# Scan of a hybrid backbone: the unit matrix and r are scaled on GpSimd and added on VectorE, not by identity products

## Chip, core and metric

One core of a Trainium2 chip runs the whole program. The metric is the device time of one execution in microseconds (us), the median of several runs. PE is the tensor engine (its weight loads are listed apart, as PEld), DVE the vector engine, ACT the scalar engine, POOL is GpSimd and SP issues DMAs.

## What is computed

Two trunk layers of a diffusion backbone over 512 latent and 256 context tokens of width 1024. Layer 0 has an RWKV-7 time mixer in both directions beside a windowed attention, layer 1 two kinds of attention; each layer has a squared-ReLU MLP. The change touches only the scan of the RWKV-7 mixer, which for each of 8 heads and 2 directions keeps a 64x64 state:

```python
def rwkv7_scan(f, d, s0, reverse):
    def step(state, inp):
        r_t, w_t, k_t, v_t, kk_t, a_t = inp
        sa = jnp.einsum('bhvk,bhk->bhv', state, -kk_t)
        state = (state * w_t[:, :, None, :] + sa[..., None] * (kk_t * a_t)[:, :, None, :]
                 + v_t[..., None] * k_t[:, :, None, :])
        return state, jnp.einsum('bhvk,bhk->bhv', state, r_t)
```

## The kernel before

The scan runs in chunks of 64 tokens: 12 chunks (4 of context, 8 latent), taken forwards and backwards at once, and two heads side by side on the 128 partitions, so there are four head pairs. For one pair, `prep` (lines 843 to 985) makes the factors of all chunks: AR holds four 64-column parts for each chunk (a of both directions, r of both directions, scaled by cumulative decays), BK the matching b and k, wc the decay over a whole chunk (one column for each, with one more column in front), and XI the inverse of a triangular matrix. That inverse is found on VectorE by 31 steps of two operations (lines 954 and 955, "the solver") and a merge on TensorE.

`chunks` (lines 989 to 1168) then makes one pass over the pair, in four blocks of NB = 3 chunks. In an iteration b, the helpers take turns between two neighbouring blocks: factors(b), local(b-1), masked(b), passed(b-1), own(b), step(b-1, 0), solved(b), step(b-1, 1), step(b-1, 2).

- `factors` transposes BK into BT, a into the right half of XA and v into Z; a copy of v (vr) is made in parts by ScalarE and GpSimd first.
- `masked` forms a·k (AK, masked on VectorE, line 1053) and the right half of BT (masked on VectorE, line 1060).
- `own` multiplies AK with v, `solved` multiplies by XI and overwrites the right half of XA with the solved a.
- `local` makes each chunk's own output (into py) and own state N.
- `passed` makes, for each chunk, M and Q, with which the state is passed on and read: M = 1 + (solved a)·b and Q = r + (solved a)·k, each then scaled by the chunk's decay wc along the row. The 1 and the r come into PSUM as products with the identity (lines 1110 and 1111: the constant i2, two 64x64 unit matrices on top of each other, and AR's r), in one accumulation with the products of XA and BT (line 1114); a helper `chain` keeps all of these in order on TensorE (its matmuls are recorded at lines 1012 and 1015). VectorE then reads PSUM, multiplies by wc and writes the tile MQ (line 1116). The first chunk of all has no state before it, so in a pass's first block only two of three chunks are done.
- `step` carries the state over a chunk with M (line 1131), adds N (line 1133), and adds the state's output with Q into py (line 1138).

The passes run one behind another, and a caller draws from three generators by rates: the pass, the preparation of the pairs behind it together with the output of the pair before (`mix_out`), and `ada`, which streams 512 KB pieces of modulation weights through TensorE (line 353). Each engine serves its own queue in order; how the queues are ordered was settled when the program was built, from the order in the code and from what is ready when. Tiles of one name share buffers: AK has one, MQ, XA, BT and Z have two each; AR, BK, XI and wc have one for each of two neighbouring pairs. On GpSimd run the copies of v (line 1038), the products with k (lines 940 and 947), the powers for norms (line 264, called from `pow_mhalf`), and the solver's unit matrix (lines 930 and 931).

Of the kernel before, what the change touches and what calls it, by code (L numbers as in the profile page):

```python
# [11 lines left out]
F32 = mybir.dt.float32  # L12
F32R = mybir.dt.float32r
AF = mybir.ActivationFunctionType
ALU = mybir.AluOpType
# [159 lines left out]
def trunk(ctx: ExitStack, tc: tile.TileContext, xT, cT, vec_d, wada, we, wo_in, wout, wf1, wf2, lw2_d, la2_d, lg2_d,  # L175
          rpb_d, con_d, nm_d, rot_d, out):
    nc = tc.nc
    V, S, G, PE = nc.vector, nc.scalar, nc.gpsimd, nc.tensor
    tt, ts, stt = V.tensor_tensor, V.tensor_scalar, V.scalar_tensor_tensor

    def act(o, i, f=AF.Copy, **k):
        return S.activation(o, i, f, **k)  # L182
# [12 lines left out]
    C = {k: con[:, s] for k, s in CON.items() if k != "tri"}  # L195
    VV = {k: vec[:, s] for k, s in VEC.items()}
    ident = C["ident"]
# [645 lines left out]
    def prep(p, R, rt, iv, sts, res):  # L843
# [4 lines left out]
        k = rt.tile([128, T], F32, name="k")  # L848
# [41 lines left out]
        XI = st.tile([128, NCH, 2, 64], F32, name="XI")  # L890
        xv = XI.rearrange("p c h t -> p (c h) t")
        wc = st.tile([128, 2, NCH + 1], F32, name="wc")

        AR = st.tile([128, NCH, 4, 64], F32, name="ar")
        BK = [st.tile([128, NCH, 128], F32, name=f"bk{d}") for d in range(2)]
# [25 lines left out]
        for d in range(2):  # L921
            for b in range(2):
                o = d * 64 + b * 32
                i0 = d * 48 + b * 24
# [25 lines left out]
        for s in range(31):  # L950
            a, b = s + 1, 31 - s
# [10 lines left out]
        for d in range(2):  # L962
            for b in range(2):
                o = d * 64 + b * 32
                i0 = d * 48 + b * 24
# [21 lines left out]
    NB = 3  # L987

    def chunks(p, y, ct, pch, res):
# [5 lines left out]
        AR, BK, XI, wc, kds = res[p]  # L995
        half = lambda q: slice(q * 64, q * 64 + 64)
# [5 lines left out]
        pd = pch.tile([128, 128], F32, name="pd")  # L1002
        yp = py[:, :, 0:384].rearrange("p h (c f) -> p h c f", f=64)
        B = [{} for _ in range(NCH // NB)]
        last = None
        env = {}

        def chain(*a, **k):

            nonlocal last  # L1010
            if last is None:
                last = PE.matmul(*a, **k)
            else:
                with tc.issue_after(last.ins):
                    last = PE.matmul(*a, **k)  # L1015

        def factors(b):

            pt = wide()[:, 0:NB * 256].rearrange("p (x h k) -> p h x k", x=2 * NB, h=2)
            BT = B[b]["BT"] = ct.tile([128, 2, 2 * NB, 128], F32, name="BT", bufs=2)  # L1020
            for d in range(2):
                for i in range(NB):
                    PE.transpose(pt[:, :, d * NB + i], BK[d][:, ch[d][NB * b + i], :], ident)
            act(BT[:, :, :, 0:64], pt)
            XA = B[b]["XA"] = ct.tile([128, NB, 2, 128], F32, name="XA", bufs=2)
            pw = wide()
            pt = pw[:, 0:NB * 128].rearrange("p (i h k) -> p i h k", i=NB, h=2)
            for i in range(NB):
                PE.transpose(pt[:, i], AR[:, NB * b + i, 0:2].rearrange("p d t -> p (d t)"), ident)
            pv = pw[:, 512:512 + NB * 128].rearrange("p (i f) -> p i f", i=NB)  # L1030
            vr = ct.tile([128, NB, 2, 64], F32, name="vr")
            c0 = BWD[NB * b + NB - 1]
            act(vr[:, ::-1, 0, ::-1], c3(v)[:, c0:c0 + NB])

            n = min(NB, max(4 - NB * b, 0)) or NB
            for i0, i1 in ((0, n), (n, NB)):
                if i0 < i1:
                    G.tensor_copy(vr[:, i0:i1, 1], c3(v)[:, FWD[NB * b + i0]:FWD[NB * b + i0] + i1 - i0])
            for i in range(NB):
                PE.transpose(pv[:, i], vr[:, i].rearrange("p d t -> p (d t)"), ident)  # L1040
            act(XA[:, :, :, 64:128], pt)
            Z = B[b]["Z"] = ct.tile([128, NB, 2, 2, 64], F32, name="Z", bufs=2)
            for d in range(2):
                act(Z[half(1 - d), :, d].rearrange("p i h v -> p i (h v)"), pv[half(1 - d)])
# [17 lines left out]
        def own(b):  # L1062

            AK, Z, XA = (B[b][x] for x in ("AK", "Z", "XA"))
            px = wide()[:, 0:NB * 128].rearrange("p (i h v) -> p i h v", i=NB, h=2)
            for i in range(NB):
                for h, d in HD:
                    PE.matmul(px[half(d), i, h], AK[half(1 - d), h, i], Z[half(1 - d), i, d, h], start=True, stop=True)
            act(XA[:, :, :, 0:64], px)

# [33 lines left out]
        def passed(b):  # L1104

            BT, XA = B[b]["BT"], B[b]["XA"]
            i0 = 0 if b else 1
            pm = wide().rearrange("p (d x) -> p d x", d=2)[:, :, 0:NB * 128].rearrange("p d (i k) -> p d i k", i=NB)
            for d in range(2):
                chain(pm[:, d, i0:, 0:64], ident, C["i2"].unsqueeze(1).to_broadcast([128, NB - i0, 64]), start=True, stop=False)  # L1110
                chain(pm[:, d, i0:, 64:128], ident, AR[:, NB * b + i0:NB * b + NB, 2 + d], start=False, stop=False)
            for i in range(i0, NB):
                for h, d in HD:
                    chain(pm[half(h), d, i], XA[half(d), i, h, 64:128], BT[half(d), h, d * NB + i], start=False, stop=i == NB - 1)
            MQ = B[b]["MQ"] = ct.tile([128, 2, NB, 128], F32, name="MQ", bufs=2)
            tt(MQ[:, :, i0:], pm[:, :, i0:], wc[:, :, NB * b + i0:NB * b + NB].unsqueeze(3).to_broadcast([128, 2, NB - i0, 128]), op=ALU.mult)

        X = None

# [350 lines left out]
    with ExitStack() as p2:  # L1470
# [28 lines left out]
        for p in range(4):  # L1499
# [32 lines left out]
            t = None  # L1532
# [215 lines left out]
    with ExitStack() as p3:  # L1748
# [13 lines left out]
        with pool("po", 1) as pp:  # L1762
            ws = [W.take() for _ in range(4)]
            po = [pp.tile([128, T], F32, name=f"po{m}") for m in range(6)]
            for ms, gs in ((range(4), GROUPS[:2]), ((4, 5), GROUPS[:2]), ((0, 1), GROUPS[2:])):
                for c, tok in gs:
                    while c == 1 and pend:
                        tick()
                    for m in ms:
                        if m == len(ws):  # L1770
                            ws.append(W.take())
                        p = product(ws[m], *u1, tok.start, tok.stop, 12)
# [119 lines left out]
```

## Time and profile before

| | us |
|---|---|
| median of 3 runs | 2055.58 |
| lowest and highest of them | 2053.28, 2057.93 |
| the profiled execution | 2050.14 |
| its span, first to last instruction | 2048.3 |
| the scan's four passes, in the span | about 352 to 692 |

The profile shows one execution. Its summary gives busy times by engine; a table by windows gives them by stage; lists of groups, of waits and a timeline give single instructions; the chain of waits follows the work that ended last back from the end. An fp32 product of the code appears as two records on PE and two weight loads on PEld. The tile b is the PSUM tile of the scan's products. An activation of ScalarE appears under line 182, whoever calls it. Not all records are there: a few matmuls can be missing.

### The profile page before, as it was taken

What the parts mean: (1) busy time and instruction counts of PE and PEld (TensorE: products, weight loads), DVE (VectorE), ACT (ScalarE), POOL (GpSimd) and SP (SyncE); (2) the same over time, 40 slices, a digit from 0 to 9 for tenths busy, and PEclk for the clock granted to TensorE, in tenths of its full rate; (3) what the DMA queues carried; (4) which work ended last, traced back from release to release, by engine and by line L of the source; (5) the groups of instructions that cost most, each with busy time, mean ns of one, the idle gap of its engine ahead of it and who ended that gap; (6) DMA issues with size and microseconds to landing.
All of it is one profiled execution on the core that took longest, in us unless ns stands there. A gap on an engine that the chain in (4) does not pass through costs nothing.

```text
span 2048.3 us, 38617 instructions
## 1 busy us (share of the span) xinstructions
PE 1929.7 (94%) x16412; PEld 1630.5 (80%) x16412; DVE 1124.1 (55%) x1999; ACT 816.5 (40%) x1531; POOL 124.1 (6%) x149
## 2 busy tenths in 40 slices
PE   5999989888888899999999999899999899999997
PEld 3878767565666898888888889898878798888887
DVE  6576477467465387233444345856575575444445
ACT  3466443434335354311322122435686654222332
POOL 1000011011100000000000000001021000000000
PEclk9999989988999999999999999999999999999998
DMA  7512334675744234211221021342111334222321
GB/s 311 162 52 78 108 116 148 205 200 190 199 134 138 71 121 133 72 53 41 83 72 62 32 83 42 103 153 67 58 32 37 124 113 165 93 83 82 100 86 42
DMA packets 112013, 217.47 MB, mean 106 GB/s; under 512 B 38496, under 2 KB 63968, under 8 KB 111328
## 3 DMA queue, kind: packets, MB, share of 16 engines
q1 hardware_dynamic: 96544, 191.66, 29.2%
q10 hardware_dynamic: 15296, 23.33, 3.2%
q8 instruction: 129, 2.11, 0.4%
q14 instruction: 44, 0.36, 0.1%
HBM read 184.29 MB, written 28.05 MB: 104 GB/s over the span
## 4 chain that ended last, share of the span: by engine, by line
PE 61%; DVE 5%; ACT 3%; issue 2%; DMA 2%; POOL 1%; POOLq 0%; ACTq 0%; DVEq 0%; SPq 0%
PE x L1589 46%; PE x L430 5%; PE ax L530 2%; PE ax L511 2%; PE b L493 1%; PE b L494 1%; PE b L1015 1%; DMA w_raw<-in_wada_dram 1%; PE b L1077 1%; DVE nacc L288 1%; PE ad L353 0%; ACT P L182 0%; DVE h L310 0%; ACT w_hi L182 0%; ACT Z L182 0%
## 5 line engine op out<-in xcount | busy, mean ns | idle before, releaser
L182 ACT ACTIVATE w_hi<-w_raw 128x1024 fp32r<-128x1024 f32 x183 | 192.3, 1058 | 480.7 <-PE x L1589 367.5
L225 DVE TENSOR_TENSOR w_lo<-w_raw,w_hi 128x1024 fp32r<-128x1024 f32 x181 | 220.9, 1223 | 196.1 <-ACT w_hi L182 194.4
L1589 PE MATMUL x<-fl,w_hi 128*128 128x256 f32 (+1 forms) x864 | 291.5, 339 | 3.9 <-DVE fl L1676 3.9
L1589 PE MATMUL x<-uh,w_hi 128*128 128x512 f32 (+1 forms) x864 | 287.6, 338 | 3.0 <-ACT uh L182 3.0
L1589 PE MATMUL x<-fh,w_lo 128*128 128x256 f32 (+1 forms) x864 | 289.8, 337 | 0.0
L1589 PE MATMUL x<-ul,w_hi 128*128 128x512 f32 (+1 forms) x864 | 287.9, 336 | 0.0
L1589 PE MATMUL x<-uh,w_lo 128*128 128x512 f32 (+1 forms) x864 | 287.5, 336 | 0.0
L1589 PE MATMUL x<-fh,w_hi 128*128 128x256 f32 (+1 forms) x864 | 287.3, 338 | 0.0
L1603 DVE TENSOR_TENSOR oa<-x,oa 128x512 f32<-128x512 f32 (+1 forms) x184 | 103.1, 563 | 207.6 <-PE x L1589 206.9
L430 PE MATMUL x<-uh,w_hi 128*128 128x256 f32 (+1 forms) x560 | 190.3, 340 | 1.0 <-ACT po L182 0.7
L430 PE MATMUL x<-uh,w_lo 128*128 128x256 f32 (+1 forms) x560 | 189.1, 338 | 0.0
L430 PE MATMUL x<-ul,w_hi 128*128 128x256 f32 (+1 forms) x560 | 188.3, 336 | 0.0
L1589 PEld LDWEIGHTS x<-fl,w_hi 128*128 128x128 f32 x864 | 165.0, 191 | 22.0 <-DVE fl L1676 4.5
L1589 PEld LDWEIGHTS x<-uh,w_hi 128*128 128x128 f32 x864 | 162.4, 190 | 21.2 <-ACT uh L182 3.9
L1589 PEld LDWEIGHTS x<-fh,w_lo 128*128 128x128 f32 x864 | 164.8, 191 | 17.8
L1589 PEld LDWEIGHTS x<-fh,w_hi 128*128 128x128 f32 x864 | 162.5, 190 | 19.9 <-ACT fh L182 2.5
L1589 PEld LDWEIGHTS x<-ul,w_hi 128*128 128x128 f32 x864 | 163.0, 190 | 17.7
L1589 PEld LDWEIGHTS x<-uh,w_lo 128*128 128x128 f32 x864 | 162.9, 189 | 17.6
L430 PEld LDWEIGHTS x<-uh,w_hi 128*128 128x128 f32 x560 | 107.6, 192 | 12.0 <-issue 2.7
L430 PEld LDWEIGHTS x<-uh,w_lo 128*128 128x128 f32 x560 | 107.7, 192 | 9.5 <-issue 1.2
L430 PEld LDWEIGHTS x<-ul,w_hi 128*128 128x128 f32 x560 | 107.8, 192 | 9.3 <-issue 1.3
L1675 DVE TENSOR_TENSOR rl<-rl 128x512 f32<-128x512 f32 (+1 forms) x108 | 59.3, 551 | 77.7 <-ACT fh L182 77.5
(304 smaller groups left out, 3388.7 us busy)
## 6 DMA issues: line engine op xcount, KB each, us to landing
w_raw<-in_wf_dram SPq DMA_DIRECT2D x128, 512.0 KB
w_raw<-in_wada_dram SPq DMA_DIRECT2D x96, 512.0 KB
w_raw<-in_we_dram SPq DMA_DIRECT2D x21, 512.0 KB
w_raw<-in_wo_in_dram SPq DMA_DIRECT2D x18, 512.0 KB
w_raw<-in_wout_dram SPq DMA_DIRECT2D x16, 512.0 KB
hsc<-h ACTq DMA_DIRECT2D x8, 1024.0 KB
scr<-po ACTq DMA_DIRECT2D x21, 384.0 KB
h<-hsc SPq DMA_DIRECT2D x7, 1024.0 KB
```

The source lines that it names most:

```text
L182: return S.activation(o, i, f, **k)
L225: eng.tensor_tensor(o_lo, x, o_hi.bitcast(F32), op=ALU.subtract)
L288: V.tensor_reduce(acc, sq.rearrange("p k t -> p t k"), axis=AX.X, op=ALU.add)
L430: PE.matmul(ps[:, 0:b - a], x, y, start=j == 0, stop=j == len(pairs) - 1)
L493: PE.matmul(ps[:, off:off + n], qs, kh, start=True, stop=False)
L494: PE.matmul(ps[:, off:off + n], qs, kl, start=False, stop=True)
L511: PE.transpose(pt[:, (kb - k0) * 128:(kb - k0 + 1) * 128], P[:, kb * 128:(kb + 1) * 128], ident)
L530: PE.matmul(po[h * 64:h * 64 + 64, 0:128], v(h, k), pts[h][:, k], start=k == 0, stop=k == n - 1)
L1015: last = PE.matmul(*a, **k)
L1589: PE.matmul(o, a, b, start=n == 0, stop=n == len(pairs) - 1)
L1603: tt(oa[:, m, tok], ps, oa[:, m, tok], op=ALU.add)
L1675: tt(r, r, r, op=ALU.mult)
```

## The change

The products with the identity go, and with them the helper `chain`. GpSimd gets three operations for each block, at the start of the block in `factors`: a times wc into a new tile, which takes its turn in AK's buffer and is transposed in place of a; the unit matrix times wc into the left halves of MQ; r times wc into its right halves. MQ is so taken up one iteration earlier than before. In `passed` TensorE makes only the products of XA and BT, already scaled by wc through a, and VectorE adds MQ to them and writes MQ. The first column of wc, which nobody read before, is set to 1.

```diff
--- before.py
+++ after.py
@@ -890,6 +890,7 @@
         XI = st.tile([128, NCH, 2, 64], F32, name="XI")
         xv = XI.rearrange("p c h t -> p (c h) t")
         wc = st.tile([128, 2, NCH + 1], F32, name="wc")
+        G.memset(wc[:, :, 0:1], 1.0)
 
         AR = st.tile([128, NCH, 4, 64], F32, name="ar")
         BK = [st.tile([128, NCH, 128], F32, name=f"bk{d}") for d in range(2)]
@@ -1002,17 +1003,7 @@
         pd = pch.tile([128, 128], F32, name="pd")
         yp = py[:, :, 0:384].rearrange("p h (c f) -> p h c f", f=64)
         B = [{} for _ in range(NCH // NB)]
-        last = None
         env = {}
-
-        def chain(*a, **k):
-
-            nonlocal last
-            if last is None:
-                last = PE.matmul(*a, **k)
-            else:
-                with tc.issue_after(last.ins):
-                    last = PE.matmul(*a, **k)
 
         def factors(b):
 
@@ -1022,11 +1013,19 @@
                 for i in range(NB):
                     PE.transpose(pt[:, :, d * NB + i], BK[d][:, ch[d][NB * b + i], :], ident)
             act(BT[:, :, :, 0:64], pt)
+
+            aw = ct.tile([128, NB, 2, 64], F32, name="AK")
+            w_ = wc[:, :, NB * b:NB * b + NB].unsqueeze(3).to_broadcast([128, 2, NB, 64])
+            di = lambda x: x.rearrange("p i d t -> p d i t")
+            G.tensor_tensor(di(aw), di(AR[:, NB * b:NB * b + NB, 0:2]), w_, op=ALU.mult)
+            IR = B[b]["MQ"] = ct.tile([128, 2, NB, 128], F32, name="MQ", bufs=2)
+            G.tensor_tensor(IR[:, :, :, 0:64], C["i2"].unsqueeze(1).unsqueeze(1).to_broadcast([128, 2, NB, 64]), w_, op=ALU.mult)
+            G.tensor_tensor(IR[:, :, :, 64:128], di(AR[:, NB * b:NB * b + NB, 2:4]), w_, op=ALU.mult)
             XA = B[b]["XA"] = ct.tile([128, NB, 2, 128], F32, name="XA", bufs=2)
             pw = wide()
             pt = pw[:, 0:NB * 128].rearrange("p (i h k) -> p i h k", i=NB, h=2)
             for i in range(NB):
-                PE.transpose(pt[:, i], AR[:, NB * b + i, 0:2].rearrange("p d t -> p (d t)"), ident)
+                PE.transpose(pt[:, i], aw[:, i].rearrange("p d t -> p (d t)"), ident)
             pv = pw[:, 512:512 + NB * 128].rearrange("p (i f) -> p i f", i=NB)
             vr = ct.tile([128, NB, 2, 64], F32, name="vr")
             c0 = BWD[NB * b + NB - 1]
@@ -1106,14 +1105,11 @@
             BT, XA = B[b]["BT"], B[b]["XA"]
             i0 = 0 if b else 1
             pm = wide().rearrange("p (d x) -> p d x", d=2)[:, :, 0:NB * 128].rearrange("p d (i k) -> p d i k", i=NB)
-            for d in range(2):
-                chain(pm[:, d, i0:, 0:64], ident, C["i2"].unsqueeze(1).to_broadcast([128, NB - i0, 64]), start=True, stop=False)
-                chain(pm[:, d, i0:, 64:128], ident, AR[:, NB * b + i0:NB * b + NB, 2 + d], start=False, stop=False)
             for i in range(i0, NB):
                 for h, d in HD:
-                    chain(pm[half(h), d, i], XA[half(d), i, h, 64:128], BT[half(d), h, d * NB + i], start=False, stop=i == NB - 1)
-            MQ = B[b]["MQ"] = ct.tile([128, 2, NB, 128], F32, name="MQ", bufs=2)
-            tt(MQ[:, :, i0:], pm[:, :, i0:], wc[:, :, NB * b + i0:NB * b + NB].unsqueeze(3).to_broadcast([128, 2, NB - i0, 128]), op=ALU.mult)
+                    PE.matmul(pm[half(h), d, i], XA[half(d), i, h, 64:128], BT[half(d), h, d * NB + i], start=True, stop=True)
+            MQ = B[b]["MQ"]
+            tt(MQ[:, :, i0:], pm[:, :, i0:], MQ[:, :, i0:], op=ALU.add)
 
         X = None
```

## Rows read from the trace of the kernel before

**Rows 1.** The summary: busy us (share of the span) x instructions.
```profile
PE 1929.7 (94%) x16412; PEld 1630.5 (80%) x16412; DVE 1124.1 (55%) x1999; ACT 816.5 (40%) x1531; POOL 124.1 (6%) x149
```
**Rows 2.** Busy us (x instructions) by window, one for each pass; header shows columns.
```profile
core 0: us, PE busy (x) PEld busy (x) DVE busy (x) ACT busy (x) POOL busy (x), PEclk, DMA share, GB/s
352.00:454.00 102.00, 89.48 (x1708) 61.95 (x1710) 60.16 (x133) 39.33 (x76) 11.83 (x11) 0.94 0.71 210
454.00:552.00 98.00, 87.30 (x1418) 60.54 (x1418) 55.14 (x124) 34.68 (x66) 10.36 (x11) 0.89 0.63 191
552.00:626.00 74.00, 63.62 (x1526) 49.33 (x1522) 45.07 (x107) 29.54 (x61) 7.34 (x8) 1.00 0.48 132
626.00:692.00 66.00, 56.31 (x1060) 46.95 (x1061) 30.98 (x41) 32.04 (x55) 4.95 (x5) 0.92 0.31 108
```
**Rows 3.** Waits from 352 to 692 us: total us, times, longest.
```profile
PE ad L353 <- DMA w_raw<-in_wada_dram: 9.0, 9, 1.8
PE pd L1131 <- DVE MQ L1116: 8.2, 10, 1.9
...
DVE ar L903 <- PE b L1015: 9.2, 2, 5.2
DVE y L1201 <- POOL r L264: 7.2, 3, 2.4
...
POOL vr L1038 <- PE b L1040: 85.9, 9, 24.6
```
**Rows 4.** Timeline of a block in the last pass: start, us, engine, line, operation.
```profile
674.55 0.59 PE L1015 MATMUL b<-con 128*128 128x192 f32 x2
674.64 0.96 DVE L1060 TENSOR_TENSOR BT<-b,con 128x768 f32<-128x768 f32 x1
...
676.05 0.89 PE L1015 MATMUL b<-BT,XA 64*64 64x128 f32 x24
...
677.01 0.96 DVE L1116 TENSOR_TENSOR MQ<-b,wc 128x768 f32<-128x768 f32 x1 [1.41 <-PE b L1015]
...
678.02 0.38 PE L1131 MATMUL pd<-x,MQ 64*64 64x64 f32 x5 [0.39 <-DVE MQ L1116]
```
**Rows 5.** The chain of waits: start, us, what; first, middle and last of seven.
```profile
540.06 1.18 PE b L1015 x6
...
594.81 0.42 DVE pr L954
...
607.55 2.43 PE b L1015 x32
...
682.92 2.36 PE b L1015 x32
```
**Rows 6.** Line 1015: weight loads (ns min/median/max), a first block, total by window.
```profile
L1015 PEld LDWEIGHTS b<-con x56: 186/189/337, 377.6 to 683.6; 128*128 128x128 f32 x56
...
377.15 0.49 PE L1012 MATMUL b<-con 128*128 128x128 f32 x2
...
378.24 0.67 PE L1015 MATMUL b<-BT,XA 64*64 64x128 f32 x16
...
352.00:692.00 340.00, 37.49 (x472) 29.14 (x472) 0.93 0.56 168
```
**Rows 7.** Groups on POOL, by form and by line.
```profile
L947 POOL TENSOR_TENSOR kds<-kds,t 128x768 f32<-128x768 f32 x3 | 5.5, 1836 | 3.1 <-DVE bk L942 3.1
...
L1038 POOL COPY vr<-v x20: 236/347/1402, 349.2 to 660.3; 128x192 f32<-128x192 f32 x12, 128x64 f32<-128x64 f32 x4, 128x128 f32<-128x128 f32 x4
```
**Rows 8.** Timeline of POOL and DVE side by side; then line 955 by window.
```profile
347.55 2.57 DVE L908 TENSOR_TENSOR bk<-t,ei 128x768 f32<-128x768 f32 x1
...
421.97 1.81 POOL L940 TENSOR_TENSOR t<-ic,k 128x768 f32<-128x768 f32 x1 [4.89 <-DVE bk L908]
422.01 0.95 DVE L1060 TENSOR_TENSOR BT<-b,con 128x768 f32<-128x768 f32 x1
422.88 1.10 DVE L955 TENSOR_TENSOR X<-X,pr 96x175 f32<-96x175 f32 x1
...
352.00:692.00 340.00, 32.14 (x93) 0.93 0.56 168
```

## Prediction

> **What bounds the kernel now.** I read the page's summary first: PE is busy for 94% of the span, no other compute engine for more than 55% [rows 1]. Over 2048 us that says little about one stage, so the stage that the change touches comes next. The scan (`chunks`, one pass for each of four head pairs, with the preparation of later pairs and the `ada` products woven in) fills 352 to 692 us. Cut into its four passes, PE is busy for 85 to 89% of the time, DVE for 47 to 61%, and POOL, which the change loads, for 7 to 12% [rows 2]. PE is the most loaded engine, but not full: its queue is served in order and stands idle for 43 of the 340 us (the sum of the four rows against 340), waiting for `ada` weights, for MQ on DVE, and so on [rows 3].
>
> Then one clean block in the last pass [rows 4]. After `masked`, PE runs eight records of identity products (two for each product in the code) from 674.55 to 676.05 us, then 24 records of XA with BT until 676.94. DVE multiplies by wc from 677.01 for 0.96 us, and the first product of `step` begins at 678.02. The reader is to see a chain without a gap: identity, XA with BT, MQ, `step`. The chain of waits goes through the stage in this way again and again [rows 5]. That view reaches back only to 529 us. Of the nine `passed` stages after it, seven have their products on the chain; one, at 594 us, lies beside the triangular solver on DVE, which is on the chain instead, and one is covered by lateness of ACT and DVE.
>
> **What is removed.** Four identity products in each of 16 blocks are 128 records. In the clean block eight take 676.05 - 674.55 = 1.50 us, 188 ns each, which is the time of their weight load (189 ns median). In a pass's first block, where they have 128 columns, eight go from 377.15 to 378.24, 1.09 us [rows 4, 6]. So 12 x 1.50 + 4 x 1.09 = 22.4 us of PE, out of the 37.5 us that line 1015 keeps it busy.
> The Trainium skill ("TensorE: Matmul & The Clock Gate", section "LDWEIGHTS (loading the stationary operand)") has a weight load take its number of columns divided by 1.2 GHz, 107 ns for 128. By that figure the removal would be worth 13.7 us, an estimate; the trace has 189 ns for the load, and the trace decides.
>
> How much lies on the path? The seven stages on the chain give 6 x 1.50 + 1.09 = 10.1 us. For the seven before 529 us there is no chain; I take four, 5.6 us, since DVE is nearly as loaded as PE in parts of that time; none and all seven (9.7) are the ends. What is late next in a clean block is BT's mask on DVE: it ends at 674.64 + 0.96 = 675.60, the 24 records would end at 675.45, so MQ would start at 675.62 and `step` at about 676.65 against 678.02 [rows 4]. That is 1.4 us of the 1.5, so the term is (10.1 + 5.6) x 0.93 = 14.6 us, with 9 and 20 as ends.
>
> **What replaces it on DVE.** The pass over MQ keeps its size, one operand in PSUM and one in SBUF; the broadcast wc becomes the dense MQ. BT's mask is such an operation of 768 elements and takes as long, 0.96 us [rows 4]. No cost; ends -0.1 and +0.1 us for each of 16.
>
> **What GpSimd gets.** Three operations of 384 elements in each block, 48 in all. The nearest rows: two operands of 768 elements take 1.84 us, a copy of 192 elements 0.35 [rows 7]. Half of 1.84 is 0.92; with a fixed part of 0.18, what the copies of 64 (0.24) and 192 leave for none, it is 1.0. I take 1.0, so 48 us on an engine that is busy for 34.5 of 340. As work of POOL this is hidden. Three things are not.
>
> First, **DVE beside POOL**. While POOL ran L940 from 421.97 to 423.78, BT's mask (PSUM and SBUF) took its usual 0.95 us, but the solver's X += pr, with two operands in SBUF, took 1.10 us instead of some 0.35 (32.14 us / 93) and ended just after POOL did. A product of two SBUF operands beside the L940 of the first pair took 2.57 us, where 768 elements take 0.95 [rows 8]. So a DVE operation with two SBUF operands waits for the POOL operation to finish. X += pr fills 32 us of the first three passes, its product as much: 64 of 274 us, 23%; all of DVE's work there is 160.4 us, 59% [rows 2, 8]. I take 40%, since most products of the preparation have two SBUF operands too: 36 POOL operations x 1.0 us x 0.4 = 14.4, and in the last pass, which has no solver, 12 x 0.2 = 2.4: 16.8 us of DVE. Where DVE would have been idle (two fifths of the time) such a delay is lost; where the chain runs through the solver it counts [rows 5]. I put 40% on the path: +6.7 us, ends 0 and 16.8.
> By the Trainium skill ("SBUF — State Buffer", section "SBUF: two separate sides") the pair of SBUF ports that GpSimd and VectorE share is held for a whole instruction and the loser blocks fully; the trace agrees, with the 2.57 us.
>
> Second, **waits in POOL's queue**. The scaled a uses the one buffer of AK, so it waits for `own` of the block before; `step`, `solved` and the transposes of BK lie between that and its use, more than the 1.0 us. The halves of MQ wait until `step` has read the MQ of two blocks before (two buffers), but are wanted a whole block later. So the new waits are covered themselves; what is queued behind them on POOL is the copy of v for the transposes, the powers of the norms (L264), the k products (L940, L947) and the solver's unit matrix (L930), and DVE waits for these; it does so today, for L264 alone 7.2 us in three times [rows 3]. About 0.5 us for four such operations in three passes is 6 us, a third of it on the path: +2, ends 0 and 8. The added memset of wc's first column is one tiny operation in each pass, nothing.
>
> Third, a **release that comes earlier**. AR and wc were last read by `passed` of the last block; AR's last readers are now `masked` and POOL, wc's is POOL, most of a block sooner. DVE waited twice for this before it wrote the AR of the next pair but one, 9.2 us [rows 3]. These waits go, and a few products with what hangs on them come earlier. I take -2 us, ends -9 and 0.
>
> **Sum**: -14.6 + 6.7 + 2 - 2 = -7.9 us. The profiled execution took 2050.14 us (2048.3 of span and 1.8 around it), so it would come to 2042.2; it lies 5.4 below the median of the three runs, 2055.58, and against that median the forecast is 2047.7. No DMA is added, removed or moved.
>
> **Rivals.** (a) *GpSimd's hold on DVE decides*, slower. If DVE sets the time in the three passes with a solver, each POOL operation costs what DVE's full load gives: 36 x 0.59 + 12 x 0.47 = 26.9 us, against 14.6 gained, 2 lost in the queue and 2 won by the release: +12, 2068 us. It decides from 14.6 us on the path, 0.30 us for each of 48 operations. For it: the solver on the chain. Against: the last pass has no solver, and DVE is idle for two fifths overall.
> The skill's lock, named above, is the rule of this rival; it says that DVE blocks, not how much of that is on the path.
> (b) *PE was not the limit*, no change. The transfers of `ada` weights (9.0 us of PE's idle time), the solver and the trip of `mixd` through DRAM stand where they are, and what PE saves turns into longer waits for them: 14.6 shrinks to 6.7, and the time is 2055.6. For it: those waits; against: seven of nine stages on the chain.
> (c) *The block waits for GpSimd*, slower. In the code the copies of v stand behind the three new operations. If POOL's queue has this order, the copy waits for the MQ buffer, free at the end of `step`, and then for 2 x 1.0 us before its own 0.35, of which the transposes in front of it on PE cover perhaps 1.0: 1.35 us x 12 blocks = 16 us, 2064. Against it: today POOL copies v as soon as the buffer is free, a block ahead (85.9 us of its idle time end there) [rows 3], so its order goes by what is ready.
>
> **How the numbers follow.** Forecast 0.58, (a) 0.14, (b) 0.20, (c) 0.08. The predicted time is 2047.7. With the first term at 20 and little lost to POOL the time is some 2036; the range 2036 to 2063 covers the forecast with its bounds, (b), and (c) but for its end; (a) and the rest are left out. By 0.2% (4.1 us, about what a measurement of this kernel can tell from no change), and with a little of the forecast's own spread: faster 0.57, same 0.22, slower 0.21.
>
> **What would show it.** 24 records of line 1015 in 0.9 us (16 in a first block) right behind `masked`, and `step` 1.4 us sooner after it in the last pass: the first term. X += pr at 1 us or more beside the new POOL operations, and some 14 us more of DVE in 352 to 626: the port term. Transposes on PE that wait for POOL would show (c). The L903 waits for PE gone: the release. The forecast is wrong if line 1015 shrinks and the scan ends no earlier, or if the time of other stages moves.

## The result, and the profile after

The changed kernel takes 2067.51 us (median of 22 runs, of which one, at 4943 us, is not in the ratio), the kernel before 2056.7 us in the same rounds. The ratio is 1.0056, with a 95% interval of 1.0044 to 1.0069: the change costs 11.5 us (0.0056 x 2056.7). The forecast was 2047.7 us, a gain, and 2067.5 lies above its range. The profiled execution took 2073.08 us, 2068.8 of it span.

The summary of the page, beside [rows 1]: VectorE has 8.8 us more, GpSimd 47.8 more, and TensorE, from which 22 us of products were taken, as much as before.

```profile
PE 1930.3 (93%) x16284; PEld 1625.9 (79%) x16284; DVE 1132.9 (55%) x1999; ACT 815.8 (39%) x1531; POOL 171.9 (8%) x201
```

Of the 20.5 us between the spans of the two profiled executions (2068.8 and 2048.3), 18.4 lie in the scan. To compare kernels I measure the scan from 352 us to ScalarE's copy of the last pass's y. Here is that stretch of the kernel before, as one row of the table by windows. Columns: window, length, busy us (x instructions) of PE, PEld, DVE, ACT and POOL, granted TensorE clock, DMA share, GB/s.

```profile
352.00:688.47 336.47, 293.18 (x5675) 215.24 (x5676) 189.44 (x401) 134.13 (x255) 34.49 (x35) 0.93 0.56 170
```

And the changed kernel, the same table, its four passes each from one copy of y to the next, and the sum:

```profile
352.00:450.04 98.04, 83.46 (x1623) 56.97 (x1620) 62.67 (x130) 37.83 (x74) 28.14 (x23) 0.93 0.66 207
450.04:554.48 104.44, 85.89 (x1538) 61.55 (x1535) 59.60 (x126) 37.45 (x72) 25.00 (x26) 0.82 0.60 178
554.48:638.04 83.56, 69.48 (x1501) 48.82 (x1502) 47.82 (x109) 27.71 (x58) 19.44 (x21) 0.88 0.52 149
638.04:706.89 68.85, 54.44 (x1103) 44.20 (x1099) 31.26 (x41) 33.64 (x58) 10.83 (x14) 0.83 0.31 103
sum 354.89, PE 293.26 PEld 211.53 DVE 201.35 ACT 136.63 POOL 83.40; mean PE 73.32 PEld 52.88 DVE 50.34 ACT 34.16 POOL 20.85
```

Against 336.47 us the scan takes 354.89, 18.4 more (this execution is 5.6 us above its kernel's median, that of before 6.6 below the 2056.7, so some 12 us of the difference between the two executions are spread from run to run and not the change). The reader is to see three things. PE is busy for 293 us in both, although 22 us of its work are gone; its clock fell from 0.93 to 0.86, which is more time at the lower of its two levels (1.2 in place of 2.4 GHz); the fall is not such spread alone, since over all runs the granted clock of the whole program has a median of 0.970 before (23 runs, those beside e1 below) and 0.960 after. PE's idle time grew from 43.3 to 61.6 us (length less busy). DVE is busy for 12 us more with nearly the same number of operations (401 and 405; 1999 in either whole program).

In a clean block the change does what it says. A timeline of the last pass, beside [rows 4] (columns as there):

```profile
695.67 0.89 PE L1110 MATMUL b<-BT,XA 64*64 64x128 f32 x24
695.70 0.96 DVE L1059 TENSOR_TENSOR BT<-b,con 128x768 f32<-128x768 f32 x1
696.63 0.96 DVE L1112 TENSOR_TENSOR MQ<-b,MQ 128x768 f32<-128x768 f32 x1
...
697.64 0.38 PE L1127 MATMUL pd<-x,MQ 64*64 64x64 f32 x5
```

From the start of BT's mask to the first product of `step` it is 697.64 - 695.70 = 1.94 us, where it was 678.02 - 674.64 = 3.38 [rows 4]: 1.44 us less. MQ now starts as BT's mask ends (695.70 + 0.96 = 696.66), and the products, which end at 695.67 + 0.89 = 696.56, no longer hold it up.

The waits from 352 to 707 us, beside [rows 3] (total us, times, longest):

```profile
PE ad L353 <- DMA w_raw<-in_wada_dram: 13.0, 9, 2.4
PE b L1067 <- DVE BT L1059: 8.7, 7, 3.5
PE pd L1127 <- DVE MQ L1112: 5.8, 8, 1.5
...
POOL AK L1020 <- PE b L1067: 84.2, 13, 15.1
POOL MQ L1022 <- PE py L1134: 53.3, 13, 7.8
```

And the wait for BT's mask in the kernel before:

```profile
PE b L1068 <- DVE BT L1060: 1.4, 2, 0.9
```

The wait for MQ shrank from 8.2 to 5.8 us, but that for weight pieces grew from 9.0 to 13.0, and PE now waits 8.7 us for BT's mask in place of 1.4. No wait of PE is for POOL. VectorE's waits of 9.2 us before it wrote AR [rows 3] are gone.

Where a new product of POOL and an operation of DVE with two SBUF operands meet, one waits for the other in these two places. First the solver, near 434 us:

```profile
433.55 1.00 POOL L1020 TENSOR_TENSOR AK<-ar,wc 128x384 f32<-128x384 f32 x1 [0.26 <-PE b L1067]
433.78 0.99 DVE L956 TENSOR_TENSOR X<-X,pr 96x207 f32<-96x207 f32 x1
...
435.94 0.35 DVE L956 TENSOR_TENSOR X<-X,pr 96x192 f32<-96x192 f32 x1
```

The next, smaller step of the same line took 0.35 us. Then the start of the scan, where VectorE writes the factors of a pair:

```profile
347.18 1.66 DVE L904 SCALAR_TENSOR_TENSOR ar<-kk,E 128x256 f32<-128x256 f32 x2 [0.50 <-PE x L430]
347.34 0.95 POOL L1020 TENSOR_TENSOR AK<-ar,wc 128x384 f32<-128x384 f32 x1 [11.50 <-PE x L430]
...
350.29 1.55 POOL L1022 TENSOR_TENSOR MQ<-con,wc 128x384 f32<-128x384 f32 x1
351.06 1.59 DVE L904 SCALAR_TENSOR_TENSOR ar<-kk,E 128x768 f32<-128x768 f32 x1
351.80 1.54 POOL L1023 TENSOR_TENSOR MQ<-ar,wc 128x384 f32<-128x384 f32 x1
...
353.30 2.52 POOL L941 TENSOR_TENSOR kds<-ic,k 128x768 f32<-128x768 f32 x1
...
355.85 2.55 DVE L943 TENSOR_TENSOR bk<-kds,ei 128x768 f32<-128x768 f32 x1 [1.70 <-POOL kds L941]
```

Both sides stretch: four of the five new operations of POOL, of 384 elements each, take 0.95 to 1.55 us here against 0.83 undisturbed, and the product with k (L941), which VectorE waits for, stands behind all five.

### The profile page after: what moved, and what is told of

It reads as the page before. It is cut to its first block, busy times and chain, and to the rows that moved or that the text cites. A ratio compares the mean times of both kernels' runs of the same rounds, so it can differ in the third digit from the quotient of the medians.

```text
span 2068.8 us, 38455 instructions
## 1 busy us (share of the span) xinstructions
PE 1930.3 (93%) x16284; PEld 1625.9 (79%) x16284; DVE 1132.9 (55%) x1999; ACT 815.8 (39%) x1531; POOL 171.9 (8%) x201
## 4 chain that ended last, share of the span: by engine, by line
PE 60%; DVE 5%; ACT 3%; issue 2%; DMA 2%; POOL 1%; SPq 0%; POOLq 0%; ACTq 0%; DVEq 0%
PE x L1585 45%; PE x L430 5%; PE ax L530 2%; PE ax L511 2%; PE b L493 1%; PE b L494 1%; PE b L1076 1%; DVE nacc L288 1%; DVE X L956 0%; ACT P L182 0%; DVE h L310 0%; POOL r L264 0%; ACT w_hi L182 0%; DVE pr L955 0%; DVE w_lo L225 0%
## 5 line engine op out<-in xcount | busy, mean ns | idle before, releaser
L264 POOL TENSOR_TENSOR rs<-ms,con 128x2 f32<-128x2 f32 (+1 forms) x20 | 17.9, 893 | 1092.0 <-DVE ms L273 1063.8
```

The costliest lines, as they stand in the source:

```text
L264: G.tensor_tensor(dst, src, C["mhalf"][:, :n], op=ALU.pow)
```

## Experiments

Three theories were on the table when the first three runs were made, and a fourth, W, came with their results. P: GpSimd's reads hold up VectorE (the prediction's port term, larger than forecast). Q: the new operations cost by their places in POOL's queue and by taking AK's and MQ's buffers early. C: without the identity products TensorE is granted the fast clock for less of the time. W: TensorE was not the limit, and what it saves goes into waits.

### One half alone, and the other half alone

e1_no_identity is the kernel before without the products with the identity, and nothing in their place; 1 and r are missing from its results.

```diff
-            for d in range(2):
-                chain(pm[:, d, i0:, 0:64], ident, C["i2"].unsqueeze(1).to_broadcast([128, NB - i0, 64]), start=True, stop=False)
-                chain(pm[:, d, i0:, 64:128], ident, AR[:, NB * b + i0:NB * b + NB, 2 + d], start=False, stop=False)
...
```

> The kernel before without its identity products, and nothing in their place (the 1 and the r are left out of M and Q; POOL gets nothing). Theory P (DVE operations with two SBUF operands wait for the new POOL operations, and that costs more than the identity products gave): the gain stands alone here, 2038 to 2046 against 2056.7 of before. Theory C (without the identity products the TensorE clock is granted less often at its upper level in the scan, and the rest of PE's work takes longer): the granted clock in the scan falls from 0.94 to about 0.88 and the time stays at 2050 to 2058. Theory Q (waits in POOL's queue and for shared buffers): as P, 2038 to 2046.

Measured: 2053.48 us, against 2053.2 for the kernel before; ratio 1.0002, 0.9987 to 1.0017. The removal alone is worth nothing, within 3.5 us. Time and clock came as C expected them. Its scan, and its waits (both by the views above):

```profile
352.00:696.10 344.10, 289.10 (x5631) 209.20 (x5624) 191.02 (x404) 134.96 (x259) 36.44 (x36) 0.87 0.55 168
```
```profile
PE ad L353 <- DMA w_raw<-in_wada_dram: 17.0, 12, 2.5
PE b L1068 <- DVE BT L1060: 9.5, 7, 4.0
```

Of the 22 us PE's busy time lost 4 only, while the clock fell from 0.93 to 0.87, and the waits for pieces (9.0 before) and for BT's mask (1.4 before) grew by 16 us together; PE's idle time as a whole grew by 11.7. This execution is 5.6 us above its median, so part of this is spread; over all runs the granted clock of the whole program has a median of 0.963 here, against 0.970.

e2_identity_back is the kernel after with the identity products made as before, into PSUM that the next products overwrite, so that TensorE has its old work and GpSimd the new.

```diff
+            for d in range(2):
+                chain(pm[:, d, i0:, 0:64], ident, C["i2"].unsqueeze(1).to_broadcast([128, NB - i0, 64]), start=True, stop=True)
+                chain(pm[:, d, i0:, 64:128], ident, AR[:, NB * b + i0:NB * b + NB, 2 + d], start=True, stop=True)
...
```

> The changed kernel with the identity products run as well, into the same PSUM tile, where the products of XA and BT overwrite them. P and Q: PE has 22 us more to do than in the changed kernel, so it is slower than its 2067.5, 2072 to 2085. C: the identity products bring the clock back (0.94 in the scan), and the time is at or below the changed kernel's, 2056 to 2066.

Measured: 2068.7 us, ratio 1.0068, 1.0048 to 1.0087, between the two expectations. With 1.0000, 1.0002, 1.0056 and 1.0068 the four corners are complete: with GpSimd's work or without it the identity products cost nothing beyond the intervals, and GpSimd's work costs 0.54% without them and 0.68% with them (11 to 14 us). The clock of the scan is 0.92 here and 0.86 in the kernel after, and the time is the same: C as the cause of the loss falls.

### The reads taken away

e3_pool_memset is the kernel after with GpSimd's three products replaced by memsets of the same tiles at the same places, two for each tile; the scaled a, 1 and r are missing.

```diff
-            G.tensor_tensor(di(aw), di(AR[:, NB * b:NB * b + NB, 0:2]), w_, op=ALU.mult)
+            for _ in range(2):
+                G.memset(aw, 0.0)
...
-            G.tensor_tensor(IR[:, :, :, 0:64], C["i2"].unsqueeze(1).unsqueeze(1).to_broadcast([128, 2, NB, 64]), w_, op=ALU.mult)
-            G.tensor_tensor(IR[:, :, :, 64:128], di(AR[:, NB * b:NB * b + NB, 2:4]), w_, op=ALU.mult)
+            for _ in range(2):
+                G.memset(IR, 0.0)
```

> The changed kernel with POOL's three products replaced by four memsets of zeros, two over the tile for a and two over MQ, together about as long (2.3 us for a block against 2.6), with the same waits and buffers but no SBUF operand read on POOL; so a, r and the 1 are left out of the result. P: DVE is not held any more, 2045 to 2056. C and Q: as the changed kernel, 2063 to 2070, the clock in the scan near 0.87.

Measured: 2058.56 us, ratio 1.0016, 1.0000 to 1.0033, between the two expectations. GpSimd is still busy for 70 us in the scan, VectorE for 191 as in e1. So 0.40% of the 0.56% (8 us) go with the reads, and 0.14% against e1 (3 us) stay, which lies within the intervals.

### Does the clock give the gain back?

e4_no_identity_fill adds to e1 three dead products of 512 columns ahead of each merge of the solver, where TensorE waits; e5_before_fill adds them to the kernel before; e6_identity_twice is the kernel before with each identity product made twice.

```diff
+            for _ in range(3 * (1 - q)):
+                PE.matmul(pw, ident, con[:, 0:512], start=True, stop=True)
```

> The kernel before without its identity products (as in e1), and with three dead identity products of 512 columns (1.06 us each at the upper clock) on TensorE in front of each pair's merge of the triangular inverses, where PE waits for transfers and its clock falls in e1. Theory C (the lower clock gave back what the removal saved): the time at the lower clock in the scan falls from 95 us towards 60 or less, and the time falls below e1's 2053.5, to 2038 to 2050. Theory W (waits for transfers and for DVE took the saving, the clock is a by-product): no gain, and up to 12.7 us of PE more, 2053 to 2066, whatever the clock does.

> The kernel before with the same three dead products in front of each merge. C: the 44 us at the lower clock in the scan become fewer, and the time is equal or lower than before, 2045 to 2057. W: 2054 to 2068.

> The kernel before with every identity product run twice, the second time over the first: 128 records and 22 us of PE more. C: the clock is granted more, which pays for part of it, below 2066; the time at the lower clock in the scan falls below 44 us. W, and any reading by which PE's work was simply beside the path when it was removed: it stays beside the path up to the waits it fills, then counts in full, 2060 to 2078, the clock as before.

Measured: 2057.01 (ratio 1.0009, 0.9993 to 1.0024), 2057.25 (1.0012, 0.9996 to 1.0027) and 2074.98 us (1.0102, 1.0086 to 1.0117). The filling hardly raised the clock of e1's scan (0.87 to 0.88) and won nothing, so it leaves open what a higher clock would have given; e5 tells nothing. Twice the identity cost 20.5 us for 22.4 us of work and left the clock at 0.92. So more work on TensorE counts in full, and less work counts for nothing: the kernel before stands at a corner where TensorE and something else end together. That speaks for W; it does not yet say what the something is.

### The other end: transfers of weights

g0_weights_once is the kernel before, g1_weights_once_no_identity is e1, both with the `ada` weights of the scan loaded only twice.

```diff
-                w = wa.tile([128, 2, 512], F32, name="w_raw")
-                eng.dma_start(w, todo.pop(0))
-                got.append(w)
+                p = todo.pop(0)
+                if n > 3 or len(got) < n - 1:
+                    w = wa.tile([128, 2, 512], F32, name="w_raw")
+                    eng.dma_start(w, p)
+                    got.append(w)
...
-                w = got.pop(0)
+                w = got[kp % 2] if n == 3 else got.pop(0)
```

> The kernel before, with the modulation weights that stream through the scan loaded only twice and then read again and again from the same two tiles: the transfers of the other pieces are left out, TensorE's products with them all stay, so the modulation comes out wrong. It is the baseline for the next kernel. TensorE waits 9.0 us for these pieces in the scan of the kernel before, so 2044 to 2055 is expected if the waits end there and do not merely move. By either theory the mean granted clock of the scan stays between 0.92 and 0.97.

> The same loading of the modulation weights, and the products with the identity left out with nothing in their place (so the state is passed on wrongly as well). Theory T (the time that TensorE gains without the identity is spent on waits for the weight pieces: 17.0 us of such waits without the identity against 9.0 before, and the lower clock behind them): with no transfers to wait for the removal pays, this kernel is 8 to 20 us faster than its baseline (g0), and the clock of the scan falls by less than 0.03. Theory D (the set of the scan's end is VectorE's chain, the products merely fill time): it is within 5 us of its baseline, and waits for VectorE's BT, MQ and AK take the place, as they do without the identity (BT 9.5 us against 1.4).

Measured: g0 2035.19 us (ratio 0.9903, 0.9873 to 0.9933), g1 2024.29 (0.9849, 0.9804 to 0.9893). On the same chip the runs don't overlap (2030.8 to 2037.3 and 2019.8 to 2026.6). Without the transfers the removal pays 10.9 us, where with them it paid none; theory T (the waits for pieces, and the lower clock behind them, take the saving) holds. g0 itself came out below its expectation: the pieces cost more than the 9.0 us of waits for them, in what way no run shows. Their scans, and in each the wait for BT's mask:

```profile
352.00:671.44 319.44, 283.37 (x5750) 216.34 (x5750) 192.24 (x402) 134.04 (x256) 34.73 (x35) 0.94 0.23 62
```
```profile
352.00:663.87 311.87, 261.03 (x5627) 195.96 (x5622) 189.22 (x403) 134.88 (x257) 34.09 (x35) 0.92 0.24 64
```
```profile
PE b L1070 <- DVE BT L1062: 0.9, 1, 0.9
```
```profile
PE b L1070 <- DVE BT L1062: 11.8, 9, 2.5
```

PE's busy time now falls by 22.3 us, as worked out, and its clock hardly. But 15 us of it became idle time, and the scan of this execution is 7.6 us shorter: of the pure saving a half at most is on the path even here, and PE then waits 11.8 us for BT's mask (0.9 us in g0).

### A finer fetch

k0_before_half_pieces and k1_after_half_pieces fetch the pieces in halves, into six buffers of half the size. (`half_` is true for the pieces of the scan.) (`half_` is true for the pieces of the scan.)

```diff
-                w = wa.tile([128, 2, 512], F32, name="w_raw")
+                w = wa.tile([128, 1 if half_ else 2, 512], F32, name="w_raw")
...
-        sts[1], ct, tl, wa = side("st1"), side("ct"), side("tl"), side("wa", 3)
+        sts[1], ct, tl, wa = side("st1"), side("ct"), side("tl"), side("wa", 6)
```

> The kernel before with the weight pieces of the scan in halves: 256 KB transfers into six buffers of half the size, so in the same space two and a half pieces are ahead of TensorE in place of two. The results are the same. TensorE waits 9.0 us for pieces here. If the waits for pieces are a matter of how far ahead they are fetched, 2048 to 2055; twice as many transfers on SP's queue could cost what they gain.

> The kernel after with the same halves. TensorE waits 13.0 us for pieces here and has more to gain: 2055 to 2066, and the distance to the same kernel without the change (k0) falls from 11.5 us to below 8. If the distance stays at 10 to 14, the waits for pieces are not moved by the finer fetch, and this run does not tell why.

Measured: 2069.23 us (1.0080, 1.0055 to 1.0105) and 2081.58 (1.0134, 1.0109 to 1.0159). Both expectations missed. The waits for pieces did shrink, to 5.7 and 6.2 us, but TensorE's products with them filled more time. The group of line 353 in the kernel before, and the same group (line 356) with halves:

```profile
L353 PE MATMUL ad<-w_raw,si 128*32 128x256 f32 x584 | 54.1, 423 | 10.5 <-DMA w_raw<-in_wada_dram 9.0 <-DVE mod L364 1.2
```
```profile
L356 PE MATMUL ad<-w_raw,si 128*32 128x256 f32 x584 | 78.7, 424 | 6.7 <-DMA w_raw<-in_wada_dram 5.7 <-DVE mod L369 1.0
```

The same 584 records of 423 to 424 ns covered 54.1 us with whole pieces and 78.7 us with halves, so they overlapped less. So this pair says nothing on the lookahead, and it is one more case in which work added to TensorE counts (24.6 us more, 16.5 on the time). The distance between the two is 12.4 us, as without the halves.

### The scaling on another engine

f1_scale_on_scalar has ScalarE make the scaled copies, 18 activations of 128x64 for each block.

```diff
-            G.tensor_tensor(di(aw), di(AR[:, NB * b:NB * b + NB, 0:2]), w_, op=ALU.mult)
+            for d, i in DI:
+                act(aw[:, i, d], AR[:, NB * b + i, d], scale=wi(d, i))
...
+            for d, i in DI:
+                act(IR[:, d, i, 0:64], C["i2"], scale=wi(d, i))
+                act(IR[:, d, i, 64:128], AR[:, NB * b + i, 2 + d], scale=wi(d, i))
```

> The kernel after, with the scaling of a, 1 and r made by ScalarE, 18 activations of 128x64 for each block with wc's column as the scale, in place of GpSimd's three products. The results are the same. By the theory that GpSimd's reads of SBUF hold VectorE up (8 us of the loss) and its queue and buffers cost the rest, VectorE's two-operand operations are as short as before again (ar of line 904 back from 10.9 to about 8 us in total, the solver's second operation from 379 to about 345 ns), and the time is 2054 to 2061, with 288 short activations in ScalarE's way. By the rival that any early use of AK's and MQ's buffers costs the 12 us, whoever writes them, 2064 to 2072.

Measured: 2067.7 us (1.0072, 1.0050 to 1.0094), above what was expected from P and within what the rival expected. VectorE is free again (the solver's second operation 354 ns, `ar` of line 904 at 5.0 us in total against 7.2 after), but ScalarE is busy for 201.6 us of the scan in place of 134, and a wait that was 0.2 us in the kernel before (there at line 1052) is now long:

```profile
PE b L1055 <- ACT Z L182: 11.4, 6, 2.6
```

So it doesn't tell P from Q: one price went and another came.

### The reads and the buffers apart

Now the price of GpSimd's work, without the transfers of weights so that no wait for them hides it. h0_after_weights_once is the kernel after with the weights loaded twice (the edit of g0).

> The kernel after with the modulation weights of the scan loaded only twice (the transfers of the other pieces left out, TensorE's products with them kept), beside the same two kernels without the change (2035.2) and with the identity merely taken away (2024.3). If the price of GpSimd's work, 12 to 14 us by the four kernels with all transfers, is VectorE's and does not pass through the wait for weight pieces, it stands here too: 2035 to 2040. If it too is paid in waits for pieces, it shrinks here to less than half: 2024 to 2030, and the change would be a gain without those transfers.

Measured: 2046.5 us, ratio 0.9963, 0.9948 to 0.9978. That is 0.60% above g0 and 1.14% above g1: the removal pays 11 us here and GpSimd's work costs 22 to 23, more than either expectation had it.

h1_memset_weights_once is e3 with the weights loaded twice: the buffers and GpSimd's order of after, without reads. h2_products_into_scratch is g1 with the three products of after, reads and all, written to a tile that nobody reads: no buffer is taken early, and no engine waits for them. (The pool of the weight tiles has two buffers there in place of three, of which two are used.)

```diff
...
+            for x in (di(AR[:, NB * b:NB * b + NB, 0:2]), C["i2"].unsqueeze(1).unsqueeze(1).to_broadcast([128, 2, NB, 64]), di(AR[:, NB * b:NB * b + NB, 2:4])):
+                junk = ct.tile([128, 2, NB, 64], F32, name="junk")
+                G.tensor_tensor(junk, x, w_, op=ALU.mult)
...
```

> Weights of the scan loaded twice only, no identity, and on GpSimd in place of the three products of a block four memsets into the same tiles, which read nothing from SBUF (so neither a nor 1 and r arrive); tiles and order of after stay. Without any such work it is 2024.3, with the three products 2046.5. By the theory that the reads' hold on VectorE makes most of these 22 us: 2026 to 2034. By the rival that the early turn in AK's and MQ's buffers and GpSimd's place in the pass's chain make it, whatever GpSimd does there: 2038 to 2048.

> Weights of the scan loaded twice only, no identity, and GpSimd makes the same three products with the same reads, but into a scratch tile that nobody reads, so that no engine waits for them and no buffer of AK or MQ is taken early (1 and r do not arrive). By the theory that the reads' hold on VectorE makes most of the 22 us: 2036 to 2046, with VectorE's busy time in the scan some 8 to 12 us above the 189.2 us without them. By the rival that the buffers and the chain make it: 2024 to 2031.

Measured, on one chip: h1 2027.12 us (0.9863, 0.9833 to 0.9893), h2 2049.31 us (0.9969, 0.9951 to 0.9988). With the buffers, the order and GpSimd busy for 71 us, but no reads, nothing measurable is lost against g1's 0.9849 (0.14%, within the intervals); with the reads and no buffers, all of it. So the price hangs on the reads, as P has it, and the buffers and the order, as Q has it, cost nothing that can be told from zero. The scans of h0, h1 and h2, and the solver's second operation in the first two:

```profile
352.00:682.45 330.45, 270.56 (x5631) 204.27 (x5624) 201.70 (x403) 135.34 (x258) 82.16 (x84) 0.89 0.23 61
```
```profile
352.00:665.27 313.27, 262.09 (x5597) 197.63 (x5598) 190.48 (x402) 133.76 (x256) 71.08 (x96) 0.92 0.24 64
```
```profile
352.00:686.69 334.69, 274.01 (x5641) 205.04 (x5636) 196.27 (x403) 135.87 (x259) 79.89 (x85) 0.88 0.22 60
```
```profile
L958 DVE TENSOR_TENSOR X<-X,pr 96x31 f32<-96x31 f32 (+15 forms) x93 | 37.1, 399 | 1.9
```
```profile
L958 DVE TENSOR_TENSOR X<-X,pr 96x31 f32<-96x31 f32 (+15 forms) x93 | 33.8, 363 | 1.9
```

The reading rests on h0 and h1, which differ in nothing but the products and the memsets. VectorE's waits for GpSimd are nearly the same in both (18.1 and 15.6 us in total), and its busy time is not (201.70 and 190.48).

h2 comes with a reserve: in h2 nobody waits for the scratch products, so they bunch where a pair's factors are ready, 31 with a or r and 15 with the unit matrix, and the product with k that VectorE waits for stands behind them; that wait (5.4 us in one time) is part of h2's price. VectorE's waits for GpSimd come to 26.1 us there, and its busy time is only 7.1 us above g1's, below the 8 to 12 expected, while the time lies above what P expected. In h1 the memsets stand where after has its products, and cost nothing there.

The Trainium skill ("SBUF — State Buffer", section "SBUF: two separate sides") states the exception that these runs turn on: against a VectorE operation with two SBUF inputs, the lock on the shared port pair counts only for a GpSimd operation that reads SBUF. The runs agree: 20 us (h0 against h1, 1.0%) lie between products and memsets of the same places and nearly the same length (33.9 us of memsets in h1's scan; 43.7 us of products in h0's, 36.5 if each took the 0.83 us of an undisturbed one).

## Why the prediction was wrong, step by step

**What is removed**: right as far as it is PE's work. 128 records and 22.4 us were worked out, and without the transfers PE's busy time fell by 22.3 us (283.37 to 261.03).

**How much lies on the path**: this step failed. 14.6 us were forecast, with 9 and 20 as ends; 0 was measured (e1, with 3.5 us either way), below the lower end. Its local part was right: 1.4 us in a clean block was worked out, and the timeline after has 1.44. The mistake was to take the sum of such savings for the end of the scan, because the chain led through the products. The same chain also led through transfers of weights; here are all of them between 529 and 692 us in the kernel before, with what stands ahead of the first (start, us, what):

```profile
542.92 0.61 PE ad L353 x8
543.55 5.52 DMA w_raw<-in_wada_dram
...
554.97 5.48 DMA w_raw<-in_wada_dram
...
582.38 4.19 DMA w_raw<-in_wada_dram
```

Each starts when PE has read an earlier piece (the products of line 353 end 0.02 us ahead of the first), and its 4 to 5.5 us don't shrink when PE is faster; what PE saves while a transfer runs becomes a longer wait for it. The chain of e1, in the same way, from 530 us on:

```profile
539.57 4.64 DMA w_raw<-in_wada_dram
...
544.95 5.85 DMA w_raw<-in_wada_dram
...
560.80 4.13 DMA w_raw<-in_wada_dram
...
566.19 5.44 DMA w_raw<-in_wada_dram
```

The transfers now make up 20.1 us of the chain, in place of 15.2. g0 and g1 show it by the time: take the transfers away, and 10.9 of the 14.6 us are there. Rival (b), with the transfers named in it, had this mechanism; it got a chance of 0.20 and let 6.7 us survive, where none did. The prediction's own sign of being wrong, line 1015 shorter and the scan ending no earlier, is what e1 shows.

**The clock** was not in the prediction at all. In e1 a wait cost TensorE more than its length. There (below, windows of 8 us from 448) PE waited 2.51 us for a piece and 2.02 for `xw` up to 454.8, and then ran from 456 to 464 without a gap at 0.50, the 1.2 GHz level, though busy all the time.

```profile
448.00:456.00 8.00, 3.32 (x66) 2.18 (x66) 3.00 (x7) 0.42 (x1) 2.91 (x3) 0.68 0.92 201
456.00:464.00 8.00, 8.00 (x176) 6.19 (x171) 0.00 (x0) 3.85 (x8) 0.00 (x0) 0.50 1.00 267
```

A group of eight records of line 353 takes 1.08 us at the lower level and 0.64 at the upper. The lower clock follows the waits here and adds to them; how much of the lost 14.6 us is wait and how much is clock, no run separates. As a cause by itself it was not confirmed: e2 has the higher clock and the same time as the kernel after.

**What replaces it on DVE**: right. 886 ns for each MQ before, 884 after.

**GpSimd's operations**: 1.0 us each was estimated; the three kinds took 871, 1171 and 896 ns, 42.9 us for 44 records in the scan (0.83 for the shortest). Right.

**DVE beside POOL**: the mechanism was right, the size was not. 16.8 us of VectorE's time were forecast, 40% of it on the path, 6.7. VectorE's busy time in the scan grew by 11.9 us, somewhat less than thought. But the price was 8 us with the transfers (after against e3) and 20 without (h0 against h1), not 12 x 0.4 = 4.8. The second step that failed is this 40%. I had counted idle time of VectorE as cover. The solver and the factors are long sequences that a later block waits for, and what is delayed comes back on TensorE: from h1 to h0 VectorE gained 11.2 us of busy time, PE 8.5 us with the same work (clock 0.92 to 0.89), and the scan 17.2. Rival (a) had the right mechanism and, at 2068 us, the right time, but by another sum: it kept the 14.6 us of gain and lost 26.9. Why the hold costs 8 us beside the transfers and 20 without them, no run shows; that part of it falls into time in which the scan waits for a transfer anyway is only an argument.

**Waits in POOL's queue**: +2 us forecast with 0 to 8; 0.14% (3 us) with the transfers and as much without (e3 and h1 against e1 and g1), within the intervals. Right in size. **Earlier release**: the waits of line 903 are gone, as forecast, but they are gone in e1 too, whose time is that of the kernel before; what it is worth can't be told from nothing. **Rival (c)** didn't come: no wait of TensorE is for GpSimd.

The measured sum, with all transfers: 0 for the removal, 3 for queue and buffers, 8 for the reads, 11 us; without them -11 + 3 + 20 = 12. No kernel run here beats the kernel before with all its transfers: e1, which leaves the work out altogether, is its equal, so even a free way to add 1 and r would have nothing to win beside these transfers.

## What to carry to other kernels

Taking work from the busiest engine pays only up to the next thing that ends beside it, and a kernel that leaves the work out and puts nothing in its place shows that bound ahead of the change. Work that "fills idle time" on GpSimd is not free if it reads SBUF while VectorE runs operations with two SBUF operands; count each meeting as lost on the path when VectorE's operations form a chain (here 10 to 11 us of VectorE's time cost 8 us beside the transfers and 20 without them), and look at whether GpSimd needs to read at all. When a chain of waits passes through transfers several times, as here, a saving between two of them is worth only what it moves the transfers' own start.

## What the runs showed of the hardware

Work added to and work taken from the same place of TensorE were not priced alike: +22.4 us cost 20.5 (e6), -22.4 us gave 0 (e1). GpSimd's memsets (of 768 elements in 762 ns, in h1) beside VectorE's solver left its second operation at 363 ns on average, as it is without them (362 in g1); GpSimd products of 384 elements with two SBUF operands lengthened it to 399 (h0), and one of them was itself lengthened from 0.83 to 3.66 us where VectorE's operations of that kind followed each other closely (at 441 us in the kernel after). And 584 records of 424 ns, each on 32 columns of the array, filled 54.1 us when their operands came in whole pieces and 78.7 us when they came in halves (k0); why they overlap less then was not tried.
